# Eight output products moved behind the last group's columns and chunks, and one group's norm separated from its split

## The chip, the cores and the metric

The kernel runs on one core of a Trainium2 chip. The metric is the device time of one launch, in microseconds (us). Before the change it is 1995.43 us, the median of three runs (1994.53, 1995.43 and 1997.82 us). All profile numbers come from one further execution, which the hardware profiler recorded.

The names of the engines are those of the profile: PE is TensorE (matrix products), DVE is VectorE, ACT is ScalarE, POOL is GpSimd, and SP is the engine that issues most DMAs. Each engine works through its own list of instructions strictly in order. An instruction that has to wait for another engine holds up everything behind it on its own engine.

## The reference, cut to what matters

The kernel computes one layer of a sequence model on `h`, 1024 positions of 1024 channels: a token mixer with two branches, and after it a gated MLP. The change lies in the mixer:

```python
u = h @ w_in[l]
u_glu, z, xbc, dt_raw, gate_a, gate_b = split_in(u)
y_a = conformer_branch(u_glu, ...)      # v = a*sigmoid(g); 31-tap conv; LayerNorm; silu; @ w_conv_out
y_b = ssd_branch(z, xbc, dt_raw, ...)   # state-space scan in chunks of 128 positions, 4 groups of 512 channels
mix = (sigmoid(gate_a) * y_a + sigmoid(gate_b) * y_b) @ w_o[l]
h = layer_norm(DN_ALPHA * h + mix, ...)
```

and, inside `ssd_branch`, what stands behind the scan:

```python
y = y + xh * d_skip[:, None]
yg = (y.reshape(bsz, t, SSM_DIM) * silu(z)).reshape(bsz, t, SSM_GROUPS, SSM_DIM // SSM_GROUPS)
yg = yg * rsqrt(mean(square(yg), axis=-1, keepdims=True) + RMS_EPS)     # per group
yn = yg.reshape(bsz, t, SSM_DIM) * norm_w
return yn @ w_out                                                       # 2048 -> 1024
```

So each of the four groups is normed by itself, and the output product sums over the rows of all four groups.

## The kernel before, in words

Channels lie on the 128 partitions and positions along the free axis. The 1024 positions are worked through in two halves of 512 columns (`hh` = 0 and 1, called half 1 and half 2 below). `mixers(hh)` does both branches up to their last products, `combine` the rest of the mixer, `out_proj` and the MLP follow.

Every large product is made in three passes, to keep fp32 accuracy from a narrower format (fp32r): an operand is split into a high part, which ACT makes by a copy with a cast, and a low part, which DVE makes by a subtraction. `mm3` multiplies high by high (L153), high weight by low operand (L154) and low weight by high operand (L155). For a weight tile the split is L141 (ACT) and L142 (DVE), out of a staging tile that SP loads (L139); there are three buffers of split weights, so the cast of one weight waits for the product that used the third one before it. One product of 128 output rows and 512 columns has 8 x 3 = 24 matmuls and ends in one of four PSUM banks.

`mixers(hh)` runs over the four groups `g`. For each it makes the group's columns of `u` (a product, and a four-tap convolution with silu each, `conv4`), the gate `zs`, and two tiles `v` of the conformer branch (`glu`). `ssd_group` then works through four chunks of 128 columns: PE transposes and products (L478 to L525), eight decay exponentials on ACT (L485, L492), a multiplication on POOL (L496), and the work on DVE (L500 to L546) that ends in the group's tile `xT` (in the profile: x, in the lists of instructions x4) and in the sums of squares `ssum`. It gives back `normed`, which turns the sums into a factor (a matmul with ones at L554, a square root on ACT at L555, a reciprocal on DVE at L558), scales the group's rows (L561), and splits them into the big tile `yT`: L572 on ACT, L573 on DVE. Groups 0 and 1 share one big tile, groups 2 and 3 another. For group 3 `normed` goes in two parts, 384 columns and then the last chunk's 128, so that the norm of three chunks starts before the last chunk is through. The tiles `xT` have two buffers, and so have the big tiles.

The output product of the scan is made in two passes over `yT`. `ssm_out_first` multiplies the rows of groups 0 and 1 with the first half of `w_ssm_out` (weights `w_so`), eight products of 128 output channels, and stores them in DRAM (`y_scr`). `combine` multiplies the rows of groups 2 and 3 with the second half (`w_sp`), eight products again, which take turns with eight gate products (`w_gb`); DVE adds each to the stored one (L639) and gates it (L640).

The 31-tap convolution of the conformer branch is `conv31`: 30 multiply-adds of 128x512 on DVE per tile, two tiles per group, called taps below (L436). It has a low priority (an offset of -1500), so DVE does these taps whenever nothing else is ready, and the last of them stand at the end of `mixers`. Each finished tile goes to DRAM (L445, `c_scr`), because the LayerNorm of the conformer branch, in `combine`, needs all eight: SP loads them back behind the last store (L647), POOL sums them (L652, L654), PE takes the mean over the channels (L656), and so on to the tile `sT` that the products `w_co` multiply.

What sets the order: the code is written in the order of the data flow, and a scheduler gives each engine a fixed list of instructions before the kernel runs. It goes by the code's order, the priorities (weights far ahead, `conv31` far behind, the conformer's LayerNorm 900 ahead), and its own estimate of durations. Nothing is reordered on the chip.

Of the kernel before, what the change touches and what calls it, by code (L numbers as in the profile page):

```python
# [8 lines left out]
F32 = mybir.dt.float32  # L9
F32R = mybir.dt.float32r  # L10
AF = mybir.ActivationFunctionType
ALU = mybir.AluOpType
# [4 lines left out]
P = 128  # L17
D = 1024
T = 1024
HALF = 512  # L20
# [21 lines left out]
PC_NW = PC_SD + 16  # L42
# [13 lines left out]
def kernel(  # L56
# [16 lines left out]
    V, A, G, TE, SY = nc.vector, nc.scalar, nc.gpsimd, nc.tensor, nc.sync  # L73
# [14 lines left out]
    def bank(which):  # L88
        n_ps[0] += 1
        pl, tag = (pacc, "acc") if which else (psm, "sm")  # L90
        return pl.tile([P, 512], F32, tag=tag, name=f"{tag}{n_ps[0]}")
# [9 lines left out]
    ones = statep.tile([P, P], F32, name="ones")  # L101
# [3 lines left out]
    eps = const.tile([P, 1], F32, name="eps")  # L105
# [3 lines left out]
        out=quads, in_=ident.rearrange("p (j h) -> p h j", j=4), axis=AX.X, op=ALU.add  # L109
    )  # L110
    pc = const.tile([P, PC_N + 80], F32, name="pc")
# [35 lines left out]
    def big_tile(name):  # L147
        return big.tile([P, 2, KD, HALF], F32R, tag="big", name=name)
# [305 lines left out]
    def ssd_group(pl, hh, g, xT, BT, CT, zs):  # L454
# [9 lines left out]
        ssum = pl.tile([P, HALF], F32, tag="ssum", name=f"ssum{hh}_{g}")  # L464
        for c in range(4):
            nm = f"{hh}_{g}_{c}"
            cs = slice(c * P, (c + 1) * P)
# [16 lines left out]
            for h in range(8):  # L484
                A.activation(  # L485
                    out=m[:, h, :],
                    in_=ab[:, h, :],
                    func=AF.Relu,
                    scale=-1.0,
# [57 lines left out]
                out=ssum[:, cs], in_=sq.rearrange("p i l -> p l i"), axis=AX.X, op=ALU.add  # L547
            )

        def normed(yT):  # L550
            rstd = pl.tile([P, HALF], F32, tag="rstd", name=f"rstd{hh}_{g}")
            for cs in (slice(0, 3 * P), slice(3 * P, HALF)) if g == 3 else (slice(0, HALF),):
                pv = bank(0)
                TE.matmul(pv[:, cs], ones, ssum[:, cs], start=True, stop=True)  # L554
                A.activation(  # L555
                    out=rstd[:, cs], in_=pv[:, cs], func=AF.Sqrt, bias=eps, scale=1.0 / HALF
                )
                V.reciprocal(out=rstd[:, cs], in_=rstd[:, cs])  # L558
                for i in range(4):
                    k = PC_NW + 4 * g + i  # L560
                    V.scalar_tensor_tensor(  # L561
                        out=xT[:, i, cs],
                        in0=xT[:, i, cs],
                        scalar=pc[:, k : k + 1],
                        in1=rstd[:, cs],
                        op0=ALU.mult,
                        op1=ALU.mult,
                    )
                ks = slice((g % 2) * 4, (g % 2) * 4 + 4)
                hi, lo = yT[:, 0, ks, cs], yT[:, 1, ks, cs]  # L570
                for n in (slice(0, 2), slice(2, 4)):
                    A.copy(hi[:, n], xT[:, n, cs])  # L572
                    V.tensor_tensor(  # L573
                        out=lo[:, n], in0=xT[:, n, cs], in1=hi[:, n].bitcast(F32), op=ALU.subtract
                    )

        return normed

    def ssm_out_first(pl, hh, yT):
        for j in range(8):  # L580
            w = weights(wssm[j, 0], f"so{hh}_{j}")
            ps = bank(1)
            project(ps, w, yT)
            y = pl.tile([P, HALF], F32, tag="ya", bufs=2, name=f"ya{hh}_{j}")
            A.copy(y, ps)
            SY.dma_start(y_scr[hh][j], y)

    def mixers(hh, hT):
        pre = first_columns(hh, hT, (CT_B, CT_C, CT_X))
        with pool(f"mixers{hh}") as pl:  # L590
            time_steps(pl, hh, pre[0])
            for g in range(GROUPS):
                BT = conv4(pl, hh, column(hh, hT, CT_B + g) if g else pre[1], 16 + g)
                CT = conv4(pl, hh, column(hh, hT, CT_C + g) if g else pre[2], 20 + g)
                xT = pl.tile([P, 4, HALF], F32, tag="x4", bufs=2, name=f"x4_{hh}_{g}")
                for i in range(4):
                    j = 4 * g + i
                    conv4(pl, hh, column(hh, hT, CT_X + j) if j else pre[3], j, xT[:, i, :])
                zs = z_gate(pl, hh, hT, g)
                vs = [(i, glu(pl, hh, hT, i)) for i in (2 * g, 2 * g + 1)]  # L600
                done = ssd_group(pl, hh, g, xT, BT, CT, zs)
                if g == 2:
                    ssm_out_first(pl, hh, yT)
                if g % 2 == 0:
                    yT = big_tile(f"yT{hh}_{g}")
                done(yT)
                with tc.high_priority(offset=-1500):
                    conv31(pl, hh, vs)
            for j in range(8):
                pg = bank(1)  # L610
                project(pg, weights(wcol[CT_GA + j], f"gt{hh}_{j}"), hT)
                ga = pl.tile([P, HALF], F32, tag="ya", bufs=2, name=f"gt{hh}_{j}")
                A.activation(out=ga, in_=pg, func=AF.Sigmoid)
                SY.dma_start(g_scr[hh][j], ga)
        return yT
# [498 lines left out]
    yT = mixers(0, hT)  # L1114
# [130 lines left out]
```

## Time and profile before

The profiled execution took 1994.22 us, and its span (first to last instruction) is 1992.5 us. The granted TensorE clock is 0.99 of full speed on average.

| Engine | busy, us | share of the span | instructions |
|---|---|---|---|
| PE, matmuls | 1939.0 | 97% | 9409 |
| DVE | 1697.9 | 85% | 2270 |
| ACT | 1070.2 | 54% | 1609 |
| POOL | 197.0 | 10% | 230 |

Half 1 of the mixer is the stretch from about 100 to 516 us, half 2 that from about 770 to 1176 us; each is followed by `combine`, and the MLP fills the rest of the span. Times in the views are counted from the span's start. In a timeline row the first number is the start and the second the duration of the instructions named; what stands in brackets is how long the engine stood idle ahead of them, and whose work ended that. A name is printed without its buffer number, so `w_so` is any of the eight weights of `ssm_out_first`.

### The profile page before, as it was taken

Reading aid. Unit: us, or ns where it says so; the run is one execution under the profiler, and the core shown is the slowest. Engines: PE = TensorE matmul, PEld = TensorE weight load, DVE = VectorE, ACT = ScalarE, POOL = GpSimd, SP = SyncE. Lnnn points to the kernel's source line nnn. Section 1 sums busy time; section 2 is a strip of 40 time slices with the busy share of each in tenths; the row PEclk is TensorE's granted clock in tenths of the full one; section 3 lists DMA queues with packets and bytes.
Section 4 is the critical chain, followed back from the end, with each engine's and each line's share of the span. In section 5 each row is a group of like instructions: output and inputs, shape, how many; then the busy total and the mean of one; then the engine's idle time right before and its main releaser. Section 6 shows DMA issues by size and latency. Waiting matters only on the chain.

```text
span 1992.5 us, 25553 instructions
## 1 busy us (share of the span) xinstructions
PE 1939.0 (97%) x9409; PEld 1580.8 (79%) x9409; DVE 1697.9 (85%) x2270; ACT 1070.2 (54%) x1609; POOL 197.0 (10%) x230
## 2 busy tenths in 40 slices
PE   9999999999899999999899989999999999989997
PEld 7888877888788788887688868888888888878886
DVE  7599999999786669999999987577788888879778
ACT  4676756545453266776463636355555555544432
POOL 0001010000410000101100122001000000121010
PEclk9999999999999999999899999999999999999999
DMA  5323333333465432323333353476455555488673
GB/s 210 118 96 103 109 106 129 113 124 122 163 203 195 150 116 96 106 96 106 106 127 117 127 162 120 133 284 238 153 175 185 180 174 189 163 300 304 195 232 122
DMA packets 110237, 311.20 MB, mean 156 GB/s; under 512 B 12832, under 2 KB 13344, under 8 KB 110112
## 3 DMA queue, kind: packets, MB, share of 16 engines
q1 hardware_dynamic: 91872, 256.61, 38.4%
q0 software_dynamic: 11904, 41.43, 5.8%
q10 hardware_dynamic: 6336, 11.54, 1.6%
q8 instruction: 74, 1.21, 0.2%
q14 instruction: 51, 0.42, 0.1%
HBM read 255.39 MB, written 54.13 MB: 155 GB/s over the span
## 4 chain that ended last, share of the span: by engine, by line
PE 51%; DVE 20%; issue 3%; DMA 3%; ACT 1%; DVEq 0%; POOL 0%; SPq 0%; ACTq 0%; POOLq 0%
PE acc L155 11%; PE acc L153 11%; PE acc L154 11%; DVE c L436 7%; PE sm L154 6%; PE sm L155 6%; PE sm L153 6%; DVE x L391 1%; DVE w_c L142 1%; DVE x L535 1%; DVE m L512 1%; DVE x L561 1%; DMA b_scr<-fo 1%; DVE x L543 1%; DVE xbc L391 1%
## 5 line engine op out<-in xcount | busy, mean ns | idle before, releaser
L436 DVE SCALAR_TENSOR_TENSOR c<-v,pc,c 128x512 f32<-128x512 f32 x480 | 357.7, 773 | 4.6 <-ACT c L425 3.1
L154 PE MATMUL acc<-hT,w_c 128*128 128x512 f32 x616 | 241.0, 391 | 0.0
L153 PE MATMUL acc<-hT,w_c 128*128 128x512 f32 x616 | 241.0, 391 | 0.0
L155 PE MATMUL acc<-hT,w_c 128*128 128x512 f32 x616 | 239.7, 391 | 0.3
L496 POOL TENSOR_TENSOR ce<-ce,xbc 128x1024 f32<-128x1024 f32 x28 | 75.4, 2694 | 923.3 <-ACT ce L495 832.9
L153 PEld LDWEIGHTS acc<-hT,w_c 128*128 128x128 f32 x616 | 115.7, 188 | 25.6 <-issue 1.1
L155 PEld LDWEIGHTS acc<-hT,w_c 128*128 128x128 f32 x616 | 115.7, 188 | 25.3 <-DVE w_c L142 1.3
L154 PEld LDWEIGHTS acc<-hT,w_c 128*128 128x128 f32 x616 | 115.7, 188 | 23.8 <-issue 0.2
L141 ACT CAST w_c<-st_c 128x1024 fp32r<-128x1024 f32 x80 | 84.0, 1050 | 81.8 <-PE acc L155 63.3
L142 DVE TENSOR_TENSOR w_c<-st_c,w_c 128x1024 fp32r<-128x1024 f32 x80 | 97.3, 1218 | 26.3 <-ACT w_c L141 26.1
L1032 ACT CAST w_dn<-dr 128x1024 fp32r<-128x1024 f32 (+1 forms) x73 | 68.8, 945 | 82.8 <-DMA dr<-wdown 28.1
L485 ACT ACTIVATE m<-ab,acs 128x128 f32<-128x128 f32 x256 | 78.4, 390 | 64.4 <-PE sm L517 63.9
L154 PE MATMUL sm<-h1s,w_s 128*128 128x512 f32 x264 | 102.7, 389 | 0.0
L153 PE MATMUL sm<-h1s,w_s 128*128 128x512 f32 x264 | 102.7, 389 | 0.0
L155 PE MATMUL sm<-h1s,w_s 128*128 128x512 f32 x264 | 102.2, 389 | 0.0
L1033 DVE TENSOR_TENSOR w_dn<-dr,w_dn 128x1024 fp32r<-128x1024 f32 (+1 forms) x73 | 78.6, 1087 | 3.4 <-ACT w_dn L1032 3.4
L391 DVE SCALAR_TENSOR_TENSOR x<-u,pc,x 128x512 f32<-128x512 f32 x96 | 79.0, 839 | 0.0
L155 PE MATMUL acc<-h1b,w_ue 128*128 128x512 f32 x176 | 68.9, 395 | 0.8 <-DVE w_ue L142 0.8
L153 PE MATMUL acc<-h1b,w_ue 128*128 128x512 f32 x176 | 68.8, 391 | 0.0
L154 PE MATMUL acc<-h1b,w_ue 128*128 128x512 f32 x176 | 68.6, 390 | 0.0
L153 PE MATMUL sm<-h1b,w_s 128*128 128x512 f32 x176 | 68.5, 389 | 0.0
L154 PE MATMUL sm<-h1b,w_s 128*128 128x512 f32 x176 | 68.5, 389 | 0.0
(338 smaller groups left out, 5344.8 us busy)
## 6 DMA issues: line engine op xcount, KB each, us to landing
st_c<-wcol SPq DMA_DIRECT2D x80, 512.0 KB, 3.5
ab<-acs_scr SPq DMA_DIRECT2D x32, 512.0 KB, 3.7
dr<-wdown SPq DMA_DIRECT2D x55, 256.0 KB, 5.0
st_wo<-wo SPq DMA_DIRECT2D x24, 512.0 KB, 4.0
st_ue<-wup SPq DMA_DIRECT2D x22, 512.0 KB, 3.8
first_scr<-first ACTq DMA_DIRECT2D x44, 256.0 KB, 2.4
ra<-wup SPq DMA_DIRECT2D x22, 512.0 KB, 3.5
rb<-wup SPq DMA_DIRECT2D x22, 512.0 KB, 3.6
```

The lines of the kernel that those rows point to most:

```text
L141: A.copy(w[:, 0, :], st)
L142: V.tensor_tensor(out=w[:, 1, :], in0=st, in1=w[:, 0, :].bitcast(F32), op=ALU.subtract)
L153: TE.matmul(ps, wa(0), xa(0), start=start, stop=False, skip_group_check=more)
L154: TE.matmul(ps, wa(0), xa(1), start=False, stop=False, skip_group_check=more)
L155: TE.matmul(ps, wa(1), xa(0), start=False, stop=stop, skip_group_check=more)
L391: V.scalar_tensor_tensor(out=o, in0=u[:, k : k + HALF], scalar=pc[:, wc + k : wc + k + 1], in1=o, op0=ALU.mult, op1=ALU.add,)
L436: V.scalar_tensor_tensor(out=accs[i], in0=v[:, k : k + HALF], scalar=pc[:, wc + k : wc + k + 1], in1=accs[i], op0=ALU.mult, op1=ALU.add,)
L485: A.activation(out=m[:, h, :], in_=ab[:, h, :], func=AF.Relu, scale=-1.0, bias=acs[:, c, 8 * g + h : 8 * g + h + 1],)
L496: G.tensor_tensor(out=ce, in0=ce, in1=CT[:, cs].unsqueeze(1).to_broadcast([P, 8, P]), op=ALU.mult)
L512: V.tensor_tensor(out=m, in0=m, in1=cbm.unsqueeze(1).to_broadcast([P, 8, P]), op=ALU.mult)
L1032: A.copy(w[:, 0, cs], src)
L1033: V.tensor_tensor(out=w[:, 1, cs], in0=src, in1=w[:, 0, cs].bitcast(F32), op=ALU.subtract)
```

## The change

In both halves, the eight products of `ssm_out_first` move from behind group 2's chunks to behind group 3's columns and chunks. The first big tile is therefore in use until then, and the second, `yT{hh}_3`, is taken only after the products. So `normed` is cut into two functions. `scaled()` makes the factor and scales the rows in place, in `xT`; group 2 does this where it did it before. `parts(yT)` makes the split; group 2's waits until the products are written, and group 3's norm and split follow. Group 3's norm is no longer done in two parts, but over 512 columns at once, like that of the other groups.

```diff
-        def normed(yT):
+        def scaled():
             rstd = pl.tile([P, HALF], F32, tag="rstd", name=f"rstd{hh}_{g}")
-            for cs in (slice(0, 3 * P), slice(3 * P, HALF)) if g == 3 else (slice(0, HALF),):
-                pv = bank(0)
-                TE.matmul(pv[:, cs], ones, ssum[:, cs], start=True, stop=True)
...
-                V.reciprocal(out=rstd[:, cs], in_=rstd[:, cs])
...
+            pv = bank(0)
+            TE.matmul(pv, ones, ssum, start=True, stop=True)
+            A.activation(out=rstd, in_=pv, func=AF.Sqrt, bias=eps, scale=1.0 / HALF)
+            V.reciprocal(out=rstd, in_=rstd)
+            for i in range(4):
+                k = PC_NW + 4 * g + i
+                V.scalar_tensor_tensor(
+                    out=xT[:, i, :],
...
+        def parts(yT):
+            ks = slice((g % 2) * 4, (g % 2) * 4 + 4)
+            hi, lo = yT[:, 0, ks], yT[:, 1, ks]
+            for n in (slice(0, 2), slice(2, 4)):
+                A.copy(hi[:, n], xT[:, n])
+                V.tensor_tensor(
+                    out=lo[:, n], in0=xT[:, n], in1=hi[:, n].bitcast(F32), op=ALU.subtract
+                )
...
-                done = ssd_group(pl, hh, g, xT, BT, CT, zs)
+                scaled, parts = ssd_group(pl, hh, g, xT, BT, CT, zs)
                 if g == 2:
+                    scaled()
+                    split_2 = parts
+                elif g == 3:
                     ssm_out_first(pl, hh, yT)
-                if g % 2 == 0:
                     yT = big_tile(f"yT{hh}_{g}")
-                done(yT)
+                    split_2(yT)
+                    scaled()
+                    parts(yT)
+                else:
+                    if g == 0:
+                        yT = big_tile(f"yT{hh}_{g}")
+                    scaled()
+                    parts(yT)
```

From here on the lines behind the functions stand 8 further down in the changed kernel (L656 becomes L664), and inside `scaled` and `parts` the reciprocal is L555, the scaling L558, the copy L571 and the subtraction L572.

What the scheduler makes of it is shown at three places of half 1. The first is PE behind the columns of group 1, in front of the first chunk of group 2. In a row stand the line, the operation, and what is written and read; `acc` is a PSUM bank of the large products, `sm` one of the small ones, and `xN` the number of equal rows. In the list of before, the products `w_so` begin here; the last three rows ahead of L517 are the first that read group 1's rows of `yT0_0`:

```order
L154 MATMUL acc108_2939<-yT0_0_1255,w_so0_2_2936 128x512
L155 MATMUL acc108_2939<-yT0_0_1255,w_so0_2_2936 128x512
L153 MATMUL acc106_2873<-yT0_0_1255,w_so0_0_2870 128x512
L153 MATMUL acc107_2906<-yT0_0_1255,w_so0_1_2903 128x512
L153 MATMUL acc108_2939<-yT0_0_1255,w_so0_2_2936 128x512
L517 MATMUL sm92_2665<-m0_2_0_2646,xs0_2_0_2658 64x128 x8
L525 MATMUL sm93_2674<-xsd0_2_0_2660,bt0_2_0_2662 128x512
```

In the list of the changed kernel, columns of group 3 (`w_c0_29`) stand in front of the same chunk:

```order
L155 MATMUL acc110_3063<-hT0_266,w_c0_29_3066 128x512
L517 MATMUL sm92_2665<-m0_2_0_2646,xs0_2_0_2658 64x128 x8
L525 MATMUL sm93_2674<-xsd0_2_0_2660,bt0_2_0_2662 128x512
L478 MATMUL sm94_2687<-ident_75,x4_0_2_2221 128x128 x4
L481 MATMUL sm95_2692<-ident_75,xbc0_18_2172 128x128
L482 MATMUL sm95_2692<-xbc0_22_2212,xbc0_18_2172 128x128
L153 MATMUL acc110_3063<-hT0_266,w_c0_29_3066 128x512
```

The first `w_so` product now begins 378 rows later, at row 1443 of PE's list (before: row 1065), behind the last columns of group 3.

The second place is DVE at the end of half 1, from the split of group 3 to the first work of `combine`; `c0_6` and `c0_7` are the last two tiles of the 31-tap convolution. Before:

```order
L573 TENSOR_TENSOR yT0_2_3132<-x4_0_3_3292,yT0_2_3132 128x2x384 x2
L436 SCALAR_TENSOR_TENSOR c0_7_3966<-v0_7_3700,pc_99,c0_7_3966 128x512 x2
L142 TENSOR_TENSOR w_gb0_3_4467<-st_gb0_3_4465,w_gb0_3_4467 128x1024
L436 SCALAR_TENSOR_TENSOR c0_7_3966<-v0_7_3700,pc_99,c0_7_3966 128x512
L558 RECIPROCAL rstd0_3_3939<-rstd0_3_3939 128x128
L436 SCALAR_TENSOR_TENSOR c0_7_3966<-v0_7_3700,pc_99,c0_7_3966 128x512
L561 SCALAR_TENSOR_TENSOR x4_0_3_3292<-x4_0_3_3292,pc_99,rstd0_3_3939 128x128 x4
L436 SCALAR_TENSOR_TENSOR c0_7_3966<-v0_7_3700,pc_99,c0_7_3966 128x512
L573 TENSOR_TENSOR yT0_2_3132<-x4_0_3_3292,yT0_2_3132 128x2x128 x2
L436 SCALAR_TENSOR_TENSOR c0_7_3966<-v0_7_3700,pc_99,c0_7_3966 128x512 x2
L142 TENSOR_TENSOR w_sp0_2_4501<-st_sp0_2_4499,w_sp0_2_4501 128x1024
L639 TENSOR_TENSOR mb0_0_4394<-yb0_0_4362,acc157_4364 128x512
```

The norm and split of group 3 end two taps ahead of the last tap of all (the `x2` behind the second L573), and the low part of the weight `w_sp0_2` comes behind it. In the list of the changed kernel, group 3's norm and split stand about 30 rows ahead of the last tap:

```order
L558 SCALAR_TENSOR_TENSOR x4_0_3_3023<-x4_0_3_3023,pc_99,rstd0_3_3939 128x512 x4
L436 SCALAR_TENSOR_TENSOR c0_6_3952<-v0_6_3365,pc_99,c0_6_3952 128x512
L436 SCALAR_TENSOR_TENSOR c0_7_3954<-v0_7_3431,pc_99,c0_7_3954 128x512
L142 TENSOR_TENSOR w_gb0_1_4321<-st_gb0_1_4319,w_gb0_1_4321 128x1024
L572 TENSOR_TENSOR yT0_3_3934<-x4_0_3_3023,yT0_3_3934 128x1024
L436 SCALAR_TENSOR_TENSOR c0_6_3952<-v0_6_3365,pc_99,c0_6_3952 128x512
L572 TENSOR_TENSOR yT0_3_3934<-x4_0_3_3023,yT0_3_3934 128x1024
```

Behind them 35 taps follow, mixed with five low parts of weights, and the same engine's list ends the half like this:

```order
L436 SCALAR_TENSOR_TENSOR c0_7_3954<-v0_7_3431,pc_99,c0_7_3954 128x512
L142 TENSOR_TENSOR w_sp0_2_4489<-st_sp0_2_4487,w_sp0_2_4489 128x1024
L436 SCALAR_TENSOR_TENSOR c0_6_3952<-v0_6_3365,pc_99,c0_6_3952 128x512
L436 SCALAR_TENSOR_TENSOR c0_7_3954<-v0_7_3431,pc_99,c0_7_3954 128x512 x11
L647 TENSOR_TENSOR mb0_0_4382<-yb0_0_4350,acc156_4352 128x512
L648 TENSOR_TENSOR mb0_0_4382<-mb0_0_4382,gb0_0_4316 128x512
```

So the low part of `w_sp0_2` has moved from behind the last tap to in front of the last twelve, and the last eleven taps are on one tile. Half 2 is alike: the last piece of group 3's split and the low part of `w_sp1_2` stood behind the last tap there, and both now stand in front of the last five taps.

The third place is PE at the mean matmul of the conformer's LayerNorm. It stands inside the product with `w_sp0_2` in both lists, at row 2034 before and at row 2024 after. Counted over the whole list, 10 more matmuls of 128x512 follow it in half 1 of the changed kernel than before; in half 2 (rows 4728 and 4729) 4 fewer follow it. The lists of SP (the store of the last tile, the eight loads behind it, then the loads of `y_scr`) and of POOL keep their order there, and the numbers of products, taps and splits are the same in both kernels.

26 lines of the change are left out of this document (6 added, 20 removed).

## The prediction

> **What bounds the kernel now.** I read the busy times by stretch first, since shares over the whole span mix the mixer with the MLP. The rows show half 1 of the mixer, the 18 us behind it, the products that follow, and half 2 (time, then busy time and count of each engine, then the granted clock):
>
> ```profile
> core 0: us, PE busy (x) PEld busy (x) DVE busy (x) ACT busy (x) POOL busy (x), PEclk, DMA share, GB/s
> 100.00:516.00 416.00, 402.08 (x2096) 324.42 (x2095) 414.37 (x584) 253.39 (x434) 29.08 (x11) 0.99 0.33 112
> 516.00:534.00 18.00, 18.00 (x76) 14.61 (x76) 8.45 (x8) 4.21 (x6) 10.81 (x7) 0.96 0.73 248
> 534.00:600.00 66.00, 66.00 (x290) 54.08 (x289) 58.25 (x76) 37.77 (x51) 16.90 (x17) 1.00 0.58 189
> 770.00:1176.00 406.00, 388.25 (x2066) 312.89 (x2062) 403.04 (x554) 248.35 (x399) 41.55 (x15) 0.98 0.33 111
> ```
>
> In half 1 DVE is idle for 416.00 - 414.37 = 1.6 us, in half 2 for 3.0 us. PE is idle for 13.9 and 17.8 us there. So both halves are bound by DVE, whose work is the same in number before and after. Behind each half PE is the bound (66.00 of 66.00 us).
>
> Then PE's waits, the group that leads them, and its four members in the timeline:
>
> ```profile
> PE acc L153 <- ACT yT L572: 27.1, 4, 7.8
> ```
>
> ```profile
> 301.94 1.65 PE L153 MATMUL acc<-yT,w_so 128*128 128x512 f32 x3 [7.77 <-ACT yT L572]
> 513.19 0.79 PE L153 MATMUL acc<-yT,w_sp 128*128 128x512 f32 x1 [5.86 <-ACT yT L572]
> 961.87 1.65 PE L153 MATMUL acc<-yT,w_so 128*128 128x512 f32 x3 [7.01 <-ACT yT L572]
> 1175.17 0.80 PE L153 MATMUL acc<-yT,w_sp 128*128 128x512 f32 x1 [6.44 <-ACT yT L572]
> ```
>
> These four are nearly all of PE's idle time in the halves: each time the norm and split come late, because DVE is late. The change aims at all four.
>
> What sets the end of a half is therefore the other thing that DVE finishes last, the taps. Here is the chain from the last taps to the mean matmul, in half 1 (taps, loads on SP's queue, POOL's sums, PE):
>
> ```profile
> 514.47 1.54 DVE L436 SCALAR_TENSOR_TENSOR c<-v,pc,c 128x512 f32<-128x512 f32 x2
> 516.42 3.76 SPq L647 DMA_DIRECT2D cc<-c_scr  x8
> 520.19 1.87 POOL L652 TENSOR_TENSOR stats<-cc 128x512 f32<-128x512 f32 x1 [39.28 <-DMA cc<-c_scr]
> 522.14 9.33 POOL L654 TENSOR_TENSOR stats<-stats,cc 128x512 f32<-128x512 f32 x6
> 533.63 1.02 PE L656 MATMUL sm<-stats,mean_w 128*128 128x512 f32 x2
> ```
>
> and in half 2:
>
> ```profile
> 1175.12 0.75 DVE L436 SCALAR_TENSOR_TENSOR c<-v,pc,c 128x512 f32<-128x512 f32 x1
> 1175.78 0.75 DVE L573 TENSOR_TENSOR yT<-x,yT 128x256 fp32r<-128x256 f32 x2
> 1181.53 10.19 POOL L654 TENSOR_TENSOR stats<-stats,cc 128x512 f32<-128x512 f32 x6
> 1193.88 1.02 PE L656 MATMUL sm<-stats,mean_w 128*128 128x512 f32 x2
> ```
>
> Last tap to POOL's end is 531.47 - 516.0 = 15.5 us and 1191.72 - 1175.9 = 15.8 us. PE comes to the mean matmul 2.16 us behind POOL's end in both halves (533.63 - 531.47, 1193.88 - 1191.72): PE's work and the chain of the taps end almost together. The mean matmul is the anchor of my sum: nothing passes it before the taps, the loads and POOL are through, and behind it PE only has its own remaining products to do.
>
> **The change part by part.** *The four waits.* With the first yT wait gone and the clock loss behind it (2.0 us, below), PE comes to the first product on groups 2 and 3 about 9.8 us earlier than in this row, at 489.0:
>
> ```profile
> 498.79 0.39 PE L153 MATMUL acc<-yT,w_sp 128*128 128x512 f32 x1
> ```
>
> Its operand is then there: in DVE's new list 35 taps and 5 low parts of weights follow the split, 30 us by the rows below, so it ends at 486. So all 27.1 us of waiting go. But PE then reaches the mean matmul at about 516 (533.63 less both waits, 4.2 us of clock and 8 matmuls, plus some 2 us in which the bank of the second `w_sp` product waits for ACT), and POOL ends at 531 as before: PE stands some 15 us in half 1, and about 13 in half 2, in front of the anchor. The 27 us are moved, not saved. What is left is the shift of the anchor, what follows it, and the clock.
>
> *DVE's work ahead of the last tap.* Group 3's norm goes from two parts to one. The groups of DVE rows in half 1 (count, then total and mean ns of one):
>
> ```profile
> L558 DVE RECIPROCAL rstd<-rstd 128x512 f32<-128x512 f32 x3 | 10.0, 3343 | 0.2 <-ACT rstd L555 0.2
> L561 DVE SCALAR_TENSOR_TENSOR x<-x,pc,rstd 128x512 f32<-128x512 f32 x12 | 8.2, 744 | 0.0
> L573 DVE TENSOR_TENSOR yT<-x,yT 128x1024 fp32r<-128x1024 f32 x6 | 7.2, 1218 | 0.0
> L558 DVE RECIPROCAL rstd<-rstd 128x384 f32<-128x384 f32 x1 | 2.5, 2543 | 0.0
> L561 DVE SCALAR_TENSOR_TENSOR x<-x,pc,rstd 128x384 f32<-128x384 f32 x4 | 2.2, 614 | 0.0
> L573 DVE TENSOR_TENSOR yT<-x,yT 128x768 fp32r<-128x768 f32 x2 | 1.8, 955 | 0.0
> L561 DVE SCALAR_TENSOR_TENSOR x<-x,pc,rstd 128x128 f32<-128x128 f32 x4 | 1.1, 348 | 0.0
> L558 DVE RECIPROCAL rstd<-rstd 128x128 f32<-128x128 f32 x1 | 0.9, 945 | 0.0
> ```
>
> Reciprocal 3.34 against 2.54 + 0.95; scaling 4 x 0.744 against 4 x (0.614 + 0.348); split 2 x 1.218 against 2 x 0.955 + 0.75: together -1.2 us. The rows overlap by some 0.09 us each, seven instructions fall away, so I take -0.6. Group 2's split only moves.
>
> The low part of the third `w_sp` weight, formerly behind the last tap, now stands ahead of it: +1.2 us in each half (its row is below). In half 2 the last piece of the split also stood behind the last tap and is now ahead: +0.75 us.
>
> Taps on one tile in a row are slower than taps that alternate between two:
>
> ```profile
> 418.41 3.90 DVE L436 SCALAR_TENSOR_TENSOR c<-v,pc,c 128x512 f32<-128x512 f32 x5
> 1152.17 3.39 DVE L436 SCALAR_TENSOR_TENSOR c<-v,pc,c 128x512 f32<-128x512 f32 x5
> ```
>
> 0.78 against 0.68 us. Neighbouring taps on one tile go from 13 to 10 in half 1 and from 15 to 6 in half 2: -0.3 and -0.9. DVE's few waits on a late PE in half 2, of which this is the largest, can vanish when PE is ahead: between 0 and -1.5 us, I take -0.7.
>
> ```profile
> 1085.16 2.33 DVE L436 SCALAR_TENSOR_TENSOR c<-v,pc,c 128x512 f32<-128x512 f32 x3 [0.88 <-ACT c L425]
> ```
>
> So the last tap moves by -0.6 + 1.2 - 0.3 = +0.3 in half 1, and by -0.6 + 1.2 + 0.75 - 0.9 - 0.7 = -0.3 in half 2.
>
> *Release of the anchor.* PE now waits there and starts with POOL's end instead of 2.16 us behind it: -2.0 in each half (a handover of 0.2 left).
>
> *PE's work behind the anchor.* 10 more matmuls in half 1, 4 fewer in half 2. One takes 18.00 x 0.96 / 76 = 0.227 us: +2.3 and -0.9.
>
> *The clock.* The first 6 us behind each of the four waits, with the granted clock in the third place from the end:
>
> ```profile
> 301.90:307.90 6.00, 5.96 (x31) 0.67 0.01 3
> 513.20:519.20 6.00, 5.71 (x16) 0.64 0.36 121
> 961.90:967.90 6.00, 6.00 (x36) 0.50 0.01 3
> 1175.20:1181.20 6.00, 5.71 (x16) 0.62 0.78 231
> ```
>
> The losses are 6 x (1 - clock) = 2.0, 2.2, 3.0 and 2.3 us, 9.5 in all. Ahead of the anchor they were covered; now one falls behind it in each half: +2.3 each, between 2.0 and 3.0. The Trainium skill (page "TensorE: Matmul & The Clock Gate", section "What's actually happening") has the clock at half speed until PE was busy for about 3.4 us, an estimate of 1.7 us lost per stall; by that the sum would be 1.2 us lower, but all four rows lie above it, so the measurement decides.
>
> *The rest costs nothing.* The eight stores to `y_scr` pass SP's stores of the convolution tiles in its queue, but the first load of them is due at 520 us, some 90 us behind the last store. ACT has the same copies and is busy for 253 of 416 us. Group 2's split now waits for the last `w_so` product; PE's list has 243 large matmuls and three chunks from there to 489, so it ends near 422, and DVE's list reaches the split near 437. If those 15 us of cover were gone, DVE would stall there and every later tap with it.
>
> *Sum.* Half 1: +0.3 - 2.0 + 2.3 + 2.3 = +2.9. Half 2: -0.3 - 2.0 - 0.9 + 2.3 = -0.9. Together +2.0 us on the profiled execution's 1994.2 us; that is 1.2 us below the median, so the forecast is 1995.4 + 2.0 = **1997.4 us**, no change that a measurement of this kernel can tell (0.2%, or 4 us). With the clock's and the waits' bounds, and 3 us either way for the collisions below, its own range is 1993 to 2002.
>
> **The rivals.** *The weight's wait gets into the taps' path: slower.* The low part that moves ahead of the last twelve taps (half 1) and last five (half 2) is the one that DVE waited for before:
>
> ```profile
> 519.69 1.23 DVE L142 TENSOR_TENSOR w_sp<-st_sp,w_sp 128x1024 fp32r<-128x1024 f32 x1 [3.68 <-ACT w_sp L141]
> 1181.77 2.13 DVE L142 TENSOR_TENSOR w_sp<-st_sp,w_sp 128x1024 fp32r<-128x1024 f32 x1 [5.23 <-ACT w_sp L141]
> ```
>
> Its cast needs the buffer of the third gate product to be free. If the two waits stay as long, both fall on the chain: +8.9, 2006.3 us. For it: the instruction, its cast and its predecessor are the same. Against it: by the count above that gate product ends at 489 + 48 x 0.227 = 500, the cast at 501, and DVE comes to the low part only at 506 (eleven taps at 0.78 and one before 516). It decides where PE is more than 5 us later than I count.
>
> *Fewer collisions of DVE and POOL: faster.* A POOL multiplication stretches what DVE does beside it:
>
> ```profile
> 281.70 2.75 POOL L496 TENSOR_TENSOR ce<-ce,xbc 128x1024 f32<-128x1024 f32 x1 [18.29 <-ACT ce L495]
> 282.59 2.94 DVE L142 TENSOR_TENSOR w_so<-st_so,w_so 128x1024 fp32r<-128x1024 f32 x1 [0.41 <-ACT w_so L141]
> 289.76 1.21 DVE L142 TENSOR_TENSOR w_so<-st_so,w_so 128x1024 fp32r<-128x1024 f32 x1
> ```
>
> 2.94 against 1.21 us is a stretch of 1.7. Fourteen such multiplications follow the place where the lists part (six in half 1, eight in half 2). If half of them cost such a stretch before and half of those no longer do, it is about -6, all of it on the taps: 1991. If none cost anything, -12: 1985. The new neighbours are other rows of the same kinds, which speaks for a small difference of either sign.
>
> *The waits go and nothing takes their place: much faster.* Then -27.1 - 9.5: 1958.8 us. That needs the taps to end 14 us earlier in each half, while DVE has 1.6 and 3.0 us of idle time there in all. The Trainium skill (page "Perfetto Trace Analysis", section "Optimization Strategy") advises to find the gaps on the most contended engine and to make the dependencies behind them start sooner, and to interleave regimes. Read for PE with 97%, that rule gives this rival; the rows of the stretch name DVE instead.
>
> That the change doesn't take the waits away is not open: the lists show PE with other work at both places.
>
> **How the numbers follow.** Forecast 0.55, the weight's wait or another new stall of DVE 0.22, fewer collisions 0.18, a full gain 0.05. Of the forecast's own range 0.42 lies within 4 us of 1995.4 and 0.13 above; of the collisions' 0.18, 0.15 lies below and 0.03 within. So faster 0.20, same 0.45, slower 0.35. The range of 1988.5 to 2006.5 us leaves out the full gain, about a third of the collisions' cases and some of the stalls', together near 0.17.
>
> **What would show it.** Right: no yT wait on PE; instead a wait of 13 to 16 us for POOL at L664 in both halves, half clock behind it; DVE still above 99% busy up to the last tap, which ends within 2 us of 516 and, counted from half 2's start, of 1176; the mean matmul directly behind POOL. Wrong: DVE idle for several us in a half, at L142 for `w_sp` or at the splits; the last tap more than 4 us off; or PE busy from its first `w_sp` product to the mean matmul, which would mean that the taps were not the bound.

## The result, and the profile after

The changed kernel takes 2004.83 us in the median of five runs (2003.94 to 2005.73), against 1995.43 us before (1994.53 to 1997.82): a ratio of 1.0044, with a 95% interval of 1.0029 to 1.0059. It is slower by 9.4 us, or 0.44%, clear of the noise. The profiled execution took 2003.94 us, with a span of 2001.9 us.

The page's line of busy times shows that PE and DVE, the two busiest engines, got no more work to do:

```profile
PE 1938.3 (97%) x9405; PEld 1578.4 (79%) x9405; DVE 1697.2 (85%) x2256; ACT 1088.9 (54%) x1619; POOL 199.2 (10%) x230
```

PE is busy for 0.7 us less than before, and the span is 9.4 us longer. So PE's idle time grew from 53.5 to 63.6 us, and the question is where it stands.

ACT is the exception: it is busy for 18.7 us more than before (1088.9 against 1070.2). The new order makes it load its activation tables more often, 114 times instead of 98, at 1.28 us each. At 54% of the span ACT has room for that, and DVE, which waits for ACT's results in the chunks, is idle in half 1 for no longer than before (1.5 against 1.6 us). In the mixer little of it shows in PE's waits beyond the 3.3 us for a bank in the list below.

These are PE's waits after the change (who waits, for whom; total, times, longest):

```profile
PE sm L664 <- POOL stats L662: 23.4, 2, 14.5
PE sm L517 <- DVE m L512: 5.3, 6, 1.4
PE sm L553 <- DVE ssum L546: 4.8, 5, 2.1
...
PE acc L153 <- ACT gb L635: 3.3, 2, 1.6
```

The 27.1 us of waiting for yT are gone to the last microsecond. In their place PE waits 23.4 us for POOL at the mean matmul, 3.3 us for a bank, and 7.2 us more than before for DVE inside the chunks (5.3 and 4.8 against 1.3 and 1.6): 33.9 us given back for 27.1 won. The two rows of before for the chunks are:

```profile
PE sm L554 <- DVE ssum L546: 1.6, 2, 1.3
PE sm L517 <- DVE m L512: 1.3, 2, 0.7
```

Here are the two waits at the mean matmul, in the timeline of PE, and the last taps of each half, in the timeline of DVE (the row ahead of half 1's last taps is the low part of `w_sp0_2`):

```profile
533.59 2.07 PE L664 MATMUL sm<-stats,mean_w 128*128 128x512 f32 x2 [14.51 <-POOL stats L662]
...
1198.13 2.08 PE L664 MATMUL sm<-stats,mean_w 128*128 128x512 f32 x2 [8.89 <-POOL stats L662]
```

```profile
508.18 1.22 DVE L142 TENSOR_TENSOR w_sp<-st_sp,w_sp 128x1024 fp32r<-128x1024 f32 x1
509.31 9.28 DVE L436 SCALAR_TENSOR_TENSOR c<-v,pc,c 128x512 f32<-128x512 f32 x12
...
1177.82 3.89 DVE L436 SCALAR_TENSOR_TENSOR c<-v,pc,c 128x512 f32<-128x512 f32 x5
```

The mean matmul of half 1 starts at the same time as before (533.59 against 533.63 us), though PE came to it at 519.1, and the last tap ends 2.6 us later than before (518.6 against 516.0). A table with the stages of both traces tells where the 9.4 us come up. The marks are the first and last tap of a half, the start of the mean matmul, the first column of half 2, and the last product with `w_wo`:

| Stretch | before, us | after, us | difference | forecast |
|---|---|---|---|---|
| start of the span to the first tap | 96.7 | 95.8 | -0.9 | 0 |
| half 1: first tap to last tap | 419.3 | 422.8 | +3.5 | +0.3 |
| last tap to mean matmul | 17.6 | 15.0 | -2.6 | -2.0 |
| mean matmul to half 2's first column | 146.1 | 150.8 | +4.7 | +4.6 |
| half 2: first column to last tap | 496.2 | 497.4 | +1.2 | -0.3 |
| last tap to mean matmul | 18.0 | 16.4 | -1.6 | -2.0 |
| mean matmul to the last `w_wo` product | 146.1 | 148.0 | +1.9 | +1.4 |
| the MLP, to the end of the span | 652.5 | 655.8 | +3.3 | 0 |

The last line needs a remark. The lists of DVE and ACT there are the same in both kernels, and PE's differs in the place of a few matmuls of one product. Over the thirteen profiled executions of this study, of all the kernels below too, this stretch took between 652.3 and 657.9 us. Before stands at the low end of that scatter, the changed kernel in its middle, and the runs show no cause for it in the change.

The clock behind the new waits (granted clock in the third place from the end):

```profile
core 0: us, PE busy (x), PEclk, DMA share, GB/s
533.50:539.00 5.50, 5.41 (x11) 0.51 0.51 170
...
1198.00:1204.00 6.00, 5.87 (x18) 0.75 0.51 171
```

That is 5.5 x 0.49 = 2.7 us and 6 x 0.25 = 1.5 us lost behind the two mean matmuls.

### The profile page after: what moved, and what is told of

Read it like the earlier page. It is cut to its first block, busy times and chain, and to the rows that moved or that the text cites. A ratio compares the mean times of both kernels' runs of the same rounds, so it can differ in the third digit from the quotient of the medians.

```text
span 2001.9 us, 25547 instructions
## 1 busy us (share of the span) xinstructions
PE 1938.3 (97%) x9405; PEld 1578.4 (79%) x9405; DVE 1697.2 (85%) x2256; ACT 1088.9 (54%) x1619; POOL 199.2 (10%) x230
## 4 chain that ended last, share of the span: by engine, by line
PE 53%; DVE 32%; DMA 6%; issue 5%; ACT 2%; POOL 1%; SPq 0%; DVEq 0%; ACTq 0%; POOLq 0%
DVE c L436 12%; PE acc L155 11%; PE acc L154 11%; PE acc L153 11%; PE sm L154 5%; PE sm L155 5%; PE sm L153 5%; DVE w_c L142 2%; DVE x L391 2%; DMA dr<-wdown 2%; DVE w_dn L1041 1%; DVE m L512 1%; DMA dr<-b_scr 1%; DVE x L535 1%; DVE xbc L391 1%
## 5 line engine op out<-in xcount | busy, mean ns | idle before, releaser
L436 DVE SCALAR_TENSOR_TENSOR c<-v,pc,c 128x512 f32<-128x512 f32 x480 | 364.2, 792 | 3.6 <-ACT c L425 2.5
L496 POOL TENSOR_TENSOR ce<-ce,xbc 128x1024 f32<-128x1024 f32 x28 | 80.8, 2886 | 843.6 <-ACT ce L495 843.6
```

Of the source, the lines that this page charges most:

```text
L436: V.scalar_tensor_tensor(out=accs[i], in0=v[:, k : k + HALF], scalar=pc[:, wc + k : wc + k + 1], in1=accs[i], op0=ALU.mult, op1=ALU.add,)
L496: G.tensor_tensor(out=ce, in0=ce, in1=CT[:, cs].unsqueeze(1).to_broadcast([P, 8, P]), op=ALU.mult)
```

## The experiments

### Which part of the change: the norm's form or the move

Two kernels do one part each. Here and below, a ratio compares a kernel with the kernel before on the same chip. The first is the changed kernel with group 3's norm and split in two parts again:

```diff
-                    scaled()
-                    parts(yT)
+                    for cs in (slice(0, 3 * P), slice(3 * P, HALF)):
+                        scaled(cs)
+                        parts(yT, cs)
```

> The changed kernel with group 3's norm and split in two parts again (384 and 128 columns), so the move of the eight products alone. Theory (the norm's form costs 0.6 to 0.8 us of DVE per half and is otherwise hidden, since PE waits for POOL later anyway): 0 to 3 us slower than the changed kernel, 9 to 13 us above before. Rival (the whole norm delays the split and with it PE): 3 us or more faster than the changed kernel.

Measured: 2003.85 us, 1.0043 of before (1.0027 to 1.0058), level with the changed kernel. The second is the kernel before with the norm whole:

```diff
-            for cs in (slice(0, 3 * P), slice(3 * P, HALF)) if g == 3 else (slice(0, HALF),):
+            for cs in (slice(0, HALF),):
```

> The kernel before with group 3's norm over all 512 columns at once, nothing moved. Theory (DVE bounds the halves): DVE's work shrinks by 0.7 us per half; the second yT wait of each half grows, but the anchor moves with the last tap, so the time is within 3 us of before. Rival (the two parts are what lets PE reach its w_sp products in time): the second yT waits grow by 5 us or more and all of it is seen, 8 to 12 us slower, which would make the norm's form the cause of the loss.

Measured: 1.0008 of before (0.9994 to 1.0022), no change. PE's longest waits in these two kernels, the move alone first and the norm alone second:

```profile
PE sm L673 <- POOL stats L671: 24.3, 2, 14.6
```

```profile
PE acc L153 <- ACT yT L572: 24.6, 4, 7.8
```

The move of the products alone makes the new wait, and the whole loss with it. The norm's form makes no difference that can be told from noise (0.15%, or 3 us, either way).

The second kernel shows one thing more. Its last taps end at 509.5 and 1166.8 us, 6.5 and 9.0 us earlier than before, since group 3's norm now stands behind them:

```profile
508.81 0.65 DVE L436 SCALAR_TENSOR_TENSOR c<-v,pc,c 128x512 f32<-128x512 f32 x1
...
1163.73 3.11 DVE L436 SCALAR_TENSOR_TENSOR c<-v,pc,c 128x512 f32<-128x512 f32 x4
```

The time doesn't move all the same, because PE still waits for `yT`. So an earlier last tap alone gains nothing there; the split has to come earlier too.

### Is the wait at the mean matmul the loss, and why does PE stand there

If PE waits 23.4 us at the mean matmul while some 225 further matmuls of `combine` stand behind it in its list, the loss is made by the place of that one instruction. I gave it a lower priority and changed nothing else:

```diff
                 pm = bank(0)
+            with tc.high_priority(offset=200):
                 TE.matmul(pm, mean_w, mean, start=True, stop=True)
+            with tc.high_priority(offset=900):
                 var = stats[:, 1, :]
```

> The changed kernel with one instruction given a lower priority: the mean matmul moves 47 matmuls of 128x512 down PE's list in half 1 and 42 in half 2; nothing else is changed in the code. Theory (PE's 14.5 and 8.9 us in front of the mean matmul are a loss, made by its place in PE's list): PE goes on with products until the fifth gate product needs the bank that DVE frees behind its load of y_scr (near 530 us); in half 1 some 6 us are won, in half 2 some 7 to 9: 10 to 15 us faster than the changed kernel, 1990 to 1995 us. Rival (what follows the mean matmul sets the end, and delaying it delays the end): 0 to 10 us slower than the changed kernel.

Measured: 1.0016 of before (1.0006 to 1.0025), some 5 to 6 us faster than the changed kernel (1.0044), about half of what I expected. PE's longest waits in it:

```profile
PE acc L153 <- DVE mb L647: 8.7, 2, 7.1
PE acc L155 <- DVE w_gb L142: 7.1, 2, 3.7
```

The wait for the bank is the one foreseen. It is there because DVE's first addition of `combine` waits for a load of `y_scr`, which is queued behind the eight tile loads, in this kernel as in the two others:

```profile
529.38 0.69 DVE L647 TENSOR_TENSOR mb<-yb,acc 128x512 f32<-128x512 f32 x1 [9.98 <-DMA yb<-y_scr]
```

The 7.1 us for the low part of a gate weight I had not foreseen: it stands behind that addition in DVE's list and is late with it. So the next kernel also puts the first two loads ahead:

```diff
+                with tc.high_priority(offset=1500 if j < 2 else 0):
                     SY.dma_start(ya, y_scr[hh][j])
```

> As the run with the mean matmul later (43 and 38 matmuls here), and the loads of the first two stored products stand ahead of the eight tile loads in SP's queue, so that DVE frees the banks near 522 us. Theory: the wait for the bank goes too, PE stands only 4 to 6 us in front of the mean matmul in half 1 and 0 to 2 us in half 2, 14 to 19 us faster than the changed kernel, 1986 to 1991 us. Rival: as above; or the bank was free in time, and this run is level with the one without the loads' move.

Measured: 0.9991 of before (0.9981 to 1.0002). That is half a per cent, about 10 us, below the changed kernel: less than the 14 to 19 us expected, but all that the change had lost. At the mean matmul 10.6 us of waiting are left:

```profile
PE sm L666 <- POOL stats L663: 10.6, 2, 5.9
```

The two loads have a price of their own. POOL's sums in half 1 end at 538.5 us, against 534.0 with the mean matmul later alone:

```profile
525.32 8.64 POOL L662 TENSOR_TENSOR stats<-stats,cc 128x512 f32<-128x512 f32 x6
```

```profile
527.36 11.12 POOL L663 TENSOR_TENSOR stats<-stats,cc 128x512 f32<-128x512 f32 x6
```

The first row is of the kernel with the mean matmul later, the second of the one with the loads first as well. That is part of what is missing from the expected gain.

Moving one matmul and two loads takes back what the move of the products lost, with DVE's work unchanged. So the loss hangs on where the mean matmul and these loads stand in the lists. That the scheduler put the matmul there because it reckoned the tiles ready earlier than they are on the chip is my reading of the list, not shown. Not shown either is what the two edits would bring in the kernel before; PE's list of waits there has none for POOL's sums and none for a bank behind `mb`.

A second way to end the wait is to take POOL's sums out of the chain, with eight matmuls that accumulate the mean on PE:

```diff
-                G.tensor_add(mean, cs[0], cs[1])
-                for c in cs[2:]:
-                    G.tensor_add(mean, mean, c)
                 pm = bank(0)
-                TE.matmul(pm, mean_w, mean, start=True, stop=True)
+                for i, c in enumerate(cs):
+                    TE.matmul(pm, mean_w, c, start=i == 0, stop=i == 7)
```

> The changed kernel with the conformer's sum over its eight tiles made by PE (eight accumulating matmuls with the mean's weights) in place of POOL's seven additions. Theory (PE waits at the anchor for POOL's 10.5 us): in half 1 the matmuls fit into PE's 14.5 us of waiting and the anchor ends some 7 us earlier, in half 2 with 8.9 us of waiting some 2 us earlier, and less clock is lost: 6 to 11 us faster than the changed kernel, 1994 to 1999 us. Rival (the wait at the anchor is idle time that costs nothing): 7 us of extra matmuls per half are added, 10 to 14 us slower.

> The kernel before with the same replacement. There PE does not wait for POOL (it comes to the mean matmul 2.2 us behind POOL's end), so the seven extra matmuls of about 1 us stand on PE's path: 8 to 14 us slower than before, 2004 to 2010 us. If it gets faster, PE was waiting for POOL in the kernel before too, and my reading of the anchor is wrong.

Measured: 1.0059 of before (1.0043 to 1.0075) for the changed kernel so treated, and 1.0081 (1.0063 to 1.0099) for the kernel before. The second is slower, as foreseen, by some 16 us where 8 to 14 were expected: PE had no idle time there to take the extra matmuls. The first missed. It is not faster than the changed kernel (1.0044), and whether it is slower can't be told, since the two intervals overlap. PE's timeline in half 1 and its wait in both halves say why:

```profile
523.24 9.22 PE L661 MATMUL sm<-cc,mean_w 128*128 128x512 f32 x16 [11.03 <-DMA cc<-c_scr]
```

```profile
PE sm L661 <- DMA cc<-c_scr: 16.2, 2, 11.0
```

The mean is done at 532.5 us, 3.2 us earlier than in the changed kernel (535.7). But PE comes to its eight matmuls at 512.2 us, where it came to the one at 519.1 in the changed kernel: they stand in front of some 40 more of the products in its list, in both halves. So PE again stands idle, now for the loads, and the wait falls only from 23.4 to 16.2 us. Against these 7.2 us PE is busy for 11.9 us longer (1950.2 against 1938.3). A shorter chain in front of an instruction that is placed too early, paid for with work on the busiest engine, is no gain.

### Does the loss hang on DVE

By the prediction both halves are bound by DVE, so that PE's time is only moved. If that holds, a relief of DVE must help, and the loss must shrink with it. First I took away POOL's multiplication of `ce`, which stretches DVE's work beside it (these two kernels leave out a part of the layer):

```diff
                 A.activation(out=ce, in_=ab, func=AF.Exp)
-                G.tensor_tensor(
-                    out=ce, in0=ce, in1=CT[:, cs].unsqueeze(1).to_broadcast([P, 8, P]), op=ALU.mult
-                )
```

> The changed kernel without POOL's multiplication of the tile ce (L496); the products read the unmultiplied tile, so this part of the computation is left out. Theory A (collisions: DVE operations that meet this multiplication are stretched, more of them taps in the changed kernel): no tap is stretched any more, the mean tap falls from 792 to about 745 ns, and the time falls by 25 to 39 us, the latter if DVE alone is the bound. Together with the kernel before treated alike, the distance between the two falls from 9.4 to about 4 us. Theory B (the loss lies behind the anchor: 10 more matmuls, half clock, and later stages): both kernels gain alike and the distance stays at 8 to 10 us.

> The kernel before without POOL's multiplication of the tile ce (L496); the products read the unmultiplied tile. Theory A: DVE's halves shorten by what the collisions cost, up to 34 us in all, a little less than in the changed kernel; the mean tap falls from 773 to about 745 ns; the yT waits of PE shrink. Theory B: the gain is the same as in the changed kernel.

Measured: 1978.10 us for the changed kernel (0.9906 of before, 0.9888 to 0.9923) and 1982.94 us for the kernel before (0.9930, 0.9913 to 0.9946). The order of the two is turned round: the changed kernel is now 4.8 us faster, where theory A had left it 4 us slower and theory B 8 to 10. The taps of half 1 in the four kernels (count, total and mean ns), before, changed, before without the multiplication, changed without it:

```profile
L436 DVE SCALAR_TENSOR_TENSOR c<-v,pc,c 128x512 f32<-128x512 f32 x240 | 179.6, 775 | 2.1 <-ACT c L425 1.3
```

```profile
L436 DVE SCALAR_TENSOR_TENSOR c<-v,pc,c 128x512 f32<-128x512 f32 x240 | 181.7, 789 | 1.6 <-ACT c L425 1.0
```

```profile
L436 DVE SCALAR_TENSOR_TENSOR c<-v,pc,c 128x512 f32<-128x512 f32 x240 | 171.7, 741 | 2.1 <-ACT c L425 1.3
```

```profile
L436 DVE SCALAR_TENSOR_TENSOR c<-v,pc,c 128x512 f32<-128x512 f32 x240 | 170.4, 743 | 1.6 <-ACT c L425 1.0
```

Without the multiplication, the taps of half 1 last, from first to last, 416.5 us before and 415.0 us changed; with it they last 419.3 and 422.8. So the changed kernel loses more by the collisions (taking them away gives it 1.4%, the kernel before 0.7%), and without them its last tap comes earlier than before. Yet PE still stands at its mean matmul, though this kernel is the faster of the two:

```profile
PE sm L661 <- POOL stats L659: 16.0, 2, 11.9
```

So the wait alone is not the loss; what counts is all that PE waits for, in the one order and in the other. Removing the multiplication also relieves DVE as a whole, so this pair alone does not tell the two effects apart.

The next pair relieves DVE and leaves the collisions. PE makes the groups' sums of squares, from squares that ACT writes in the narrower format, in place of DVE's reduction (L546). The lines below are the main ones; besides, two small tiles, `rstd` and `dtc`, take other buffers, and `sq` now holds a whole group:

```diff
-            sq = pl.tile([P, 4, P], F32, tag="sq", name=f"sq{nm}")
-            A.activation(out=sq, in_=xT[:, :, cs], func=AF.Square)
-            V.tensor_reduce(
-                out=ssum[:, cs], in_=sq.rearrange("p i l -> p l i"), axis=AX.X, op=ALU.add
-            )
+            A.activation(out=sq[:, :, cs], in_=xT[:, :, cs], func=AF.Square)
...
-            TE.matmul(pv, ones, ssum, start=True, stop=True)
+            for i in range(4):
+                TE.matmul(pv, ones_q, sq[:, i, :], start=i == 0, stop=i == 3)
```

> The changed kernel with the group's sums of squares made by PE (four matmuls of 128x512 with ones on rounded squares) in place of DVE's sixteen reductions per half (L546, 1.06 us each, 17 us per half). Theory (in the changed kernel DVE's taps set the anchor, and PE waits for them 14.5 and 8.9 us): most of DVE's relief is seen, 18 to 26 us faster than the changed kernel, 1979 to 1987 us, and the waits at the mean matmul fall below 6 us. Rival (the loss sits behind the anchor and in the later stages): under 5 us faster.

> The kernel before with the same replacement. Theory: the yT waits shrink, but PE has the products of groups 0 and 1 and the norms in its list where they were, so less of the relief is seen than in the changed kernel: 8 to 16 us faster than before, 1980 to 1988 us, and the changed kernel with the replacement is level or faster than this one. Rival: the gain is the same as in the changed kernel, and the distance stays near 9 us.

Measured: 1968.97 us for the changed kernel (0.9857 of before, 0.9837 to 0.9876) and 1969.31 us for the kernel before (0.9857, 0.9841 to 0.9873). Both gain more than expected, and the distance between them is gone. In the kernel before with the replacement, PE no longer waits for `yT` at all, so there the change has nothing left to win. Of the waits in question this is left in the changed kernel with the replacement:

```profile
PE sm L663 <- POOL stats L661: 4.8, 1, 4.8
```

and PE in it is busy for 1934.6 of 1966.6 us:

```profile
PE 1934.6 (98%) x9421; PEld 1580.6 (80%) x9421; DVE 1667.9 (85%) x2225; ACT 1098.1 (56%) x1626; POOL 196.8 (10%) x230
```

The replacement is nearly free on PE. Its sixteen matmuls of half 1 take 4.3 us; before, the norms of the first three groups and the larger part of the fourth took 3.1 + 0.8 = 3.9 us there. First the replacement's row, then the two of before:

```profile
L552 PE MATMUL sm<-sq,ones_q 128*128 128x512 f32 x16 | 4.3, 393 | 0.0
```

```profile
L554 PE MATMUL sm<-ssum,ones 128*128 128x512 f32 x6 | 3.1, 592 | 0.0
L554 PE MATMUL sm<-ssum,ones 128*128 128x384 f32 x2 | 0.8, 486 | 0.0
```

So DVE was the bound of the halves, and with DVE relieved the change costs nothing. It did cost time while DVE was the bound and the mean matmul stood where the scheduler had put it. With this replacement both orders are 1.4% faster than the kernel before. Each of these edits makes new lists for all engines, so the sizes of these gains are those of whole lists and not of one instruction.

The last kernel joins what had helped: squares on PE, the two loads first, the mean matmul 15 and 7 matmuls later.

> The changed kernel with the sums of squares on PE, the two loads first, and the mean matmul 15 and 7 matmuls later. Theory: of the 4.8 us that PE still waits there in half 1 some 3 go, with up to 1.5 us of clock: 2 to 5 us faster than with the squares on PE alone, 1964 to 1967 us. Rival: with DVE relieved the chain behind the mean matmul is the bound, and it is level or slower.

Measured: 0.9864 of before (0.9848 to 0.9879), level with the squares on PE alone; the expected 2 to 5 us did not come. The wait at the mean matmul is 4.5 us instead of 4.8, and the matmul itself starts 2.7 us later (523.6 against 520.9 us): the anchor moved with it, because POOL was late. POOL's first sum, which waits for the tile loads, starts 3.2 us later; first the squares on PE alone, then the joint kernel:

```profile
509.79 1.29 POOL L659 TENSOR_TENSOR stats<-cc 128x512 f32<-128x512 f32 x1 [79.10 <-DMA cc<-c_scr]
```

```profile
512.96 1.30 POOL L660 TENSOR_TENSOR stats<-cc 128x512 f32<-128x512 f32 x1 [82.59 <-DMA cc<-c_scr]
```

The last taps end at the same time in both (503.3 and 503.0 us). What differs between them is the two loads of `y_scr`, which stand ahead of the tile loads in SP's queue in the joint kernel. That these two loads are the cause fits the rows, but no run has them without the later matmul.

## Why the prediction was right, and where it was wrong

The range (1988.5 to 2006.5 us) holds the time, but that is in part luck. It reaches so far up for the rival with the weight's wait, which did not come; the forecast's own range, 1993 to 2002 us, does not hold it. The likeliest case does not either: I forecast 1997.4 us, no change that can be told from noise, with a chance of 0.45, and the kernel is clearly slower, which had 0.35. Of the signs that I had named as right, two failed: half 2's wait was to be 13 to 16 us, and half 1's last tap was to end within 2 us of 516 (it ended at 518.6). Step by step:

- *The yT waits go, and PE stands at the mean matmul instead.* Right, and the main thing. Forecast about 15 and 13 us; measured 14.5 and 8.9 us. PE came to its first product on groups 2 and 3 at 493.0 us rather than 489.0: the waits for DVE in the chunks, 7.2 us more than before in both halves together, I had set at nothing.
- *The anchor moves with the last tap.* Right in the mechanism, wrong in the size. This is the step that failed: "the last tap moves by ... +0.3 in half 1, and by ... -0.3 in half 2". Measured +3.5 and +1.2 us. The low part of the weight (+1.2 us) and the norm (11.5 us of scaling became 10.9) came as counted. The taps did not: their total rose by 2.1 us in half 1 (179.6 to 181.7) and by 4.3 us in half 2 (178.1 to 182.4), where I had set -0.3 and -0.9. In half 2 the multiplication by `zs` (L543) gave most of that back. Taking each DVE operation beside one of POOL's multiplications against the median of its kind, the stretch rose from 12.7 to 16.2 us in half 1 and from 21.0 to 22.7 in half 2.
- *Collisions.* I had them as a rival, but only in the direction of a gain; in the forecast's own range they had 3 us either way. By that count they came in the other direction, 5.2 us in all. The rows for this stood in the trace of before; I looked at the size of one collision and not at which kinds of operation are caught (the last section).
- *Release, matmuls behind the anchor, clock.* Forecast together +2.6 us in half 1 and -0.6 in half 2; the table gives +2.1 (-2.6 + 4.7) and +0.3 (-1.6 + 1.9). Right.
- *The rival with the weight's wait.* It did not come. DVE goes from the taps into that low part and out again without a gap (in the rows above, the low part at 508.18 is followed at once by the twelve taps), as the count of the gate product's end had it. The price forecast for that rival (2006.3 us) is near the measured time by accident.
- *The full gain.* It did not come, because the taps set the end, as argued. But the experiments show what I had not seen: the price is not DVE's alone. With the mean matmul further down PE's list and two loads earlier, the same DVE work ends level with before.
- *No DVE stall.* Right: DVE is idle in half 1 for 418.60 - 417.14 = 1.5 us in the changed kernel, as before.

```profile
100.00:518.60 418.60, 413.21 (x2154) 333.17 (x2153) 417.14 (x576) 262.82 (x439) 30.77 (x11) 1.00 0.34 113
```

Of the difference between the forecast (+2.0) and the measurement (+9.4), the halves up to their last taps make 4.7 us. The MLP's stretch makes another 3.3 us in the two profiled executions, which I take for scatter. On the chip of the first experiments the kernel before had a median of 1996.28 us over fifteen runs and the product move alone 2003.85, 7.6 us apart, some 2 us less, which fits that in part.

## What to carry to other kernels

A wait of an engine that is not the bound can be moved, not removed: before pricing its removal, follow what the bounding engine finishes last and see where the freed engine will stand next. Where a scheduler fixes the lists beforehand, an instruction that depends on the late engine should be placed by the measured time of what it waits for, and what frees the buffers of the work that is to fill the gap must be early too. And the larger lever was the bound itself: sixteen reductions per half taken off DVE gave 1.4%, in either order of the products.

## What the runs showed of the hardware

A multiplication on POOL does not slow all of DVE's operations beside it, only some kinds, and these it holds up until it has ended. In the kernel before, around 338 us, the four operations that read a product from PSUM (`sm`, L535) pass at 0.28 us each beside POOL, and the tap behind them, with both inputs in SBUF, takes 1.86 us instead of 0.74. It ends 0.55 us behind POOL (341.17 against 340.62):

```profile
338.28 1.11 DVE L535 SCALAR_TENSOR_TENSOR x<-x,pc,sm 128x128 f32<-128x128 f32 x4
339.31 1.86 DVE L436 SCALAR_TENSOR_TENSOR c<-v,pc,c 128x512 f32<-128x512 f32 x1
```

```profile
338.07 2.55 POOL L496 TENSOR_TENSOR ce<-ce,xbc 128x1024 f32<-128x1024 f32 x1 [13.79 <-ACT ce L495]
```

In the changed kernel, around 353 us, a low part of a weight that has begun before POOL passes in its usual 1.22 us. Of the two taps behind it, the first is held until POOL has ended, and the two take 3.55 us together, against 1.40 us for the two at 350.17:

```profile
350.17 1.40 DVE L436 SCALAR_TENSOR_TENSOR c<-v,pc,c 128x512 f32<-128x512 f32 x2
...
352.15 1.22 DVE L142 TENSOR_TENSOR w_ga<-st_ga,w_ga 128x1024 fp32r<-128x1024 f32 x1
353.28 3.55 DVE L436 SCALAR_TENSOR_TENSOR c<-v,pc,c 128x512 f32<-128x512 f32 x2
```

```profile
352.93 2.70 POOL L496 TENSOR_TENSOR ce<-ce,xbc 128x1024 f32<-128x1024 f32 x1 [16.48 <-ACT ce L495]
```

So the price of a collision depends on what the scheduler puts beside POOL: about 1.1 us where chunk work that reads PSUM fills part of the time, 2.15 us where a tap meets it at the start. The move of the eight products changed just that: taps that are held for more than 1.7 us number four in the kernel before and ten in the changed one. The Trainium skill (page "SBUF — State Buffer", section "SBUF: two separate sides") states that DVE and GpSimd share one pair of ports as an exclusive lock held for a whole instruction, and that a DVE operation needs it when it has two inputs in SBUF; the rows agree, with these durations.
